# Head sums kept ungated, a gate's rows moved from TensorE to VectorE, and two moves in order, in a two-layer retention and neighbourhood-attention block

## The chip, the core and the metric

One NeuronCore of a Trainium2 chip runs the whole program. The metric is device time in microseconds (us) of one execution; the kernel before took 1186.53 us (median of 3 runs, 1186.47 to 1189.27). Engines are called as in the profile: PE is TensorE (PEld its weight loads), DVE is VectorE, ACT is ScalarE, POOL is GpSimd, SP is SyncE, which issues most DMAs (the trace marks rows of an issuing queue with a q, as in SPq).

## The reference

Two layers work on 256 latent rows `x` and 256 context rows `ctx` of width 1024. From a condition vector each layer gets six rows of modulation per stream (shift, scale and gate, twice), as `silu(c) @ ada_w + ada_b`. Layer 0 mixes by retention with 4 heads (query and key width 256, value width 512), layer 1 by neighbourhood attention with 32 heads; each is followed by a squared-ReLU MLP of width 4096. The lines that the change bears on:

```python
mod = silu_c @ ada_w[i] + ada_b[i]
sh1, sc1, g1, sh2, sc2, g2 = jnp.split(mod, 6, axis=-1)
h = x * (1.0 + sc1) + sh1
y, yc = retention_mixer(h, hc, ...)   # sum over 4 heads of (on * silu(g)) @ w_o
x = layer_norm(DN_ALPHA * x + g1 * y, ln_g[i, 0], ln_b[i, 0])
ctx = layer_norm(DN_ALPHA * ctx + g1c * yc, ln_g[i, 0], ln_b[i, 0])
```

## The kernel before

**Matmuls.** All matmuls of weights are done as three: weights and activations are each split into a high part (`hi`, cast by ACT) and a low part (`lo = raw - hi`, subtracted by DVE), and `mm3` adds hi·hi, hi·lo and lo·hi. Weights come in units of 512 KB through a ring of 4 raw buffers; `take` (line 322) keeps up to 5 split units ahead of PE. Every DMA of weights is issued by SP, in order. Eight PSUM banks serve all matmuls.

**Start.** Eight chunks of the model width are modulated one after the other. For a chunk, `chunk_sums` (854) forms its shift and scale rows on PE, `chunk_row` (869) copies them, `chunk_turn` (888) transposes the four row tiles of `x` and `ctx` into two halves of PSUM (tile `pt`, and a part of the bank `pada` that held the rows), `chunk_columns` (874) turns the rows into columns, and `chunk_modulate` (901) writes the modulated activations `hTh` and `hTl`, for ACT and DVE half each. `turn_over` (807) issues idle matmuls on a tile of ones (`still`). The transposed `x` and `ctx` stay in `R[0..3]`, two tiles of latent and two of context rows, 128 x 1024 each.

**Retention.** The loop over 4 heads stands at line 1045. For each head: projections of q and k (`proj_T`, tiles `pq`), of v (tiles `pv`), masked scores (`pS`, with decay tables in `strips`), the output gate (`gate`, `gates`, tiles `pg`), the attention output (`po`) with its normalisation on DVE and POOL, the turn to columns (`to_oT`, tiles `pT`), and the product with the output weights (`tok_mm`, tiles `pw`), eight tiles of 128 x 512 a head. Before the change `R` is scaled by ALPHA on ACT in head 0, and `accumulate` (756) of heads 0 to 2 multiplies each `pw` by the gate row `G1` on DVE (tile `acc`) and adds it to `R` on POOL.

**Modulation in the background.** The other modulation rows come from `bg_stream` (535), a generator that loads 512 KB of `ada_w` a step (tile `rawa`) and is advanced by calls of `bg()` at fixed places in the code. For most rows a step multiplies by the condition on DVE (`weigh`, 521: four operations of 128 x 512 into spare columns of `strips`), a reduction folds the sums (`folded`, 459, tile `red`), and one small PE product finishes them (`ada_columns`, `ada_gate`, tiles `pada`). The first gate row, item `(0, 0, 2)` of the plan, is done on PE instead: `ada_mm` (440) issues four column-tiled f32 matmuls a step, eight steps, all in head 0, and the row goes to DRAM and comes back as `G1` on POOL's queue. Weighing operations keep their place in the program's order on DVE; most other instructions are ordered by a scheduler.

**Attention of layer 1.** `STEPS` (1840) is a table of 13 steps. Its first two numbers say how many weight units are fetched (cast on ACT, subtracted on DVE) before `scores(n + 2)` and `soften(n + 2)` of the step, and how many behind them; the third fetches behind `flip` and `invert`. Then come the step's own products (`K`, `Q`, `V`, tiles `pn`, `pnv`), the transposes of `flip` (tiles `ppt`, copied to `pt` by ACT and DVE in turn) and `attend` (`pav`). `soften` (1591) is four reductions on DVE (tile `mn`, custom operations in the trace, ISA in the order of instructions) and four exponentials on ACT (tile `s`). Scores are the tiles `pqk`, four banks a step.

Of the kernel before, what the change touches and what calls it, by code (L numbers as in the profile page):

```python
# [17 lines left out]
P = 128  # L18
# [86 lines left out]
def kernel(  # L105
# [323 lines left out]

    def ada_bias(l, offs, nb):  # L430
        brow = scr("brow")
        ab = ada_b[l]
        for i in range(2):
            sp.dma_start(
                out=brow[64 * i : 64 * i + 64, :nb],
                in_=bass.AP(ab.tensor, ab.offset + offs[i], [[nb, 2], [0, 32], [1, nb]]),
            )
        return brow

    def ada_mm(pr, k, nb, rhs):  # L440

        lhsT = cT[:, k, :, :].rearrange("p a t -> p (a t)")
        for j in range(4):
            pe.matmul(
                pr[32 * j : 32 * j + 32, 0:nb],
                lhsT=lhsT,
                rhs=rhs(j),
                start=(k == 0),
                stop=(k == KC - 1),
                tile_position=(0, 32 * j),  # L450
            )

    def ada_row(pr, brow, nb, p0=0, p1=P, row=None):
        if row is None:
            row = smp.tile([P, 256], F32, tag="row", name=nm("row"), bufs=1)
        dve.tensor_add(out=row[p0:p1, :nb], in0=pr[p0:p1, 0:nb], in1=brow[p0:p1, :nb])
        return row

    def folded(red, acc, t, c0, n):
# [48 lines left out]

    def on_pe(l, w, part):
        return (l, w, part) == (0, 0, 2)  # L510

    def bg_load(l, w, part, offs, n):

        if l == 1 or w == 0:
# [20 lines left out]
    def bg_stream():  # L535
# [3 lines left out]
        for l, w, part in (  # L539
            [(0, 0, 2), (0, 1, 0), (0, 1, 1), (0, 1, 2)]  # L540
            + [(1, 0, 0), (1, 0, 1), (1, 0, 2), (1, 1, 0), (1, 1, 1), (1, 1, 2)]
        ):
            sh, sc, g = 3 * w * D, (3 * w + 1) * D, (3 * w + 2) * D
            offs = (sh + 512 * part, sc + 512 * part) if part < 2 else (g, g + 512)
            for n in range(KC):
                plan.append((l, w, part, offs, n))
        nxt = bg_load(*plan[0])
        yield
        for step, (l, w, part, offs, n) in enumerate(plan):
            raw = nxt  # L550
            if step + 1 < len(plan):
                nxt = bg_load(*plan[step + 1])

            nt = 2 if l == 0 or (w == 0 and part < 2) else 1
            if on_pe(l, w, part):
                if n == 0:
                    pr = bank("pada")
                if n == KC - 2:
                    brow = ada_bias(l, offs, 256)
                ada_mm(pr, n, 256, lambda j: raw[:, j // 2, (j % 2) * 256 : (j % 2 + 1) * 256])  # L560
                if n == KC - 1:
                    row = ada_row(pr, brow, 256)
                    for t in range(2):
                        pool.dma_start(
                            out=grow[l, w][t].rearrange("(j c) -> j c", j=4), in_=row[t:P:32, :]
                        )
                yield
                continue
            if n == 0:
                red = smp.tile([P, 2, 32], F32, tag="red", name=nm("red"), bufs=2)  # L570
            if l == 0:
                dve.on = True
                for kk in range(2):
                    for t in range(nt):
                        weigh(spare(t), raw[:, kk, :], t, 2 * (n % 4) + kk, n % 4 == 0 and kk == 0)
                dve.on = False
                if n % 4 == 3:
                    yield
                    for t in range(nt):
                        folded(red, spare(t), t, 512 * (n // 4), 512)  # L580
            else:
                if n == 0:
                    acc = slot(S_VL, [P, 2, D], F32, "acc")
                for t in range(nt):

                    dve.on = n == 0 and (w, part) == (0, 0)
                    weigh(acc[:, t], raw[:].rearrange("p a n -> p (a n)"), t, n, n == 0)
                    dve.on = False
                if n == KC - 1:
                    for t in range(nt):  # L590
                        folded(red, acc[:, t], t, 0, D)
            if n == KC - 1:
                if part < 2:
                    due.append(lambda a=(l, w, red, 4 * part, nt): ada_columns(*a))
                else:
                    due.append(lambda a=(l, w, red, nt): ada_gate(*a))
            yield
# [4 lines left out]

    bg_max = [39]

# [282 lines left out]

    def chunk_turn(k):

        pts[k] = bank("pt")[:, 0:256], prs[k][:, 256:512]  # L890
        for t in range(4):
            pe.transpose(pts[k][t // 2][:, tsl(t % 2)], R[t][:, tsl(k)], ident)
# [51 lines left out]
    chunk_row(0, tsl(1))  # L944
    chunk_turn(0)
    chunk_columns(0)
    turn_over(4)
    w = ws[0]
# [71 lines left out]

    def proj_T(th, tl, first=False):
        pb = [bank("pq") for _ in range(2)]
        for u in range(2):
            ((wh, wl),) = take(1)
            for dc in range(2):
                for kk in range(4):
                    k = 4 * u + kk
                    mm3(pb[dc][:], (wh[:, kk, tsl(dc)], wl[:, kk, tsl(dc)]), hs(k, 0, NT), k == 0, k == KC - 1)
            if first:
                bg(2)  # L1030
        rotate(pb, th, tl)
# [5 lines left out]

    G1s = [None]

    def first_gate():  # L1040

        if G1s[0] is None and bg_done[0] >= 9:
            G1s[0] = load_gate(0, 0, eng=nc.gpsimd)

    for h in range(RH):
        last = h == RH - 1
        if h == 0:
# [5 lines left out]
            evac_v(pv, vh, vl)  # L1053
            act.on = True
            for a in range(2):
                act.mul(out=RR[a][:], in_=RR[a][:], mul=ALPHA)
            act.on = False
            proj_T(qkh[:, 2:4], qkl[:, 2:4], True)
        else:
            qkh = slot(S_TH, [P, 4, NT], F32R, "qkh")  # L1060
            qkl = slot(S_TL, [P, 4, NT], F32R, "qkl")
            proj_T(qkh[:, 0:2], qkl[:, 0:2])
            proj_T(qkh[:, 2:4], qkl[:, 2:4])
            vh = slot(S_VH, [P, 4, DV], F32R, "vh")
            vl = slot(S_VL, [P, 4, DV], F32R, "vl")
            pv = [bank("pv") for _ in range(4)]
            for u in range(4):
                ((wh, wl),) = take(1)
                for t in range(4):
                    for kk in range(2):  # L1070
                        k = 2 * u + kk
                        mm3(pv[t][:], hs(k, t * P, (t + 1) * P), (wh[:, kk, :], wl[:, kk, :]), k == 0, k == KC - 1)
                bg()
            evac_v(pv, vh, vl)
        qh, ql, kh, kl = qkh[:, 0:2], qkl[:, 0:2], qkh[:, 2:4], qkl[:, 2:4]

        gs = slot(S_GS, [P, 4, DV], F32, "gs")
        gu = take(4)

        def gates(ts, between=()):  # L1080

            pgs = [bank("pg") for _ in ts]
            for k in range(KC):
                wh, wl = gu[k // 2]
                for t, pg in zip(ts, pgs):
                    mm3(pg[:], hs(k, t * P, (t + 1) * P), (wh[:, k % 2, :], wl[:, k % 2, :]), k == 0, k == KC - 1)
                if h == 0 and k == 3 and len(ts) == 1:
                    bg(2)
                    first_gate()
                if k in between:  # L1090
                    between[k]()
            return pgs

        def gate(t):
            return gates((t,))[0]

# [32 lines left out]
        if h == 0:  # L1129
# [3 lines left out]
            bg()  # L1133
            first_gate()
            pg = gate(1)
            act.activation(out=gs[:, 1, :], in_=pg[:], func=AF.Silu)
        else:
            S = masked_scores()
            for t in range(2):
                pg = gate(t)  # L1140
                act.activation(out=gs[:, t, :], in_=pg[:], func=AF.Silu)
                bg()
        ons = []
        for t in range(4):
# [14 lines left out]
            if t < 2:  # L1159
                pool.tensor_mul(out=gs[:, t, :], in0=on, in1=gs[:, t, :])  # L1160
            if h == 0 and t == 0:
                bg_until(9)
                first_gate()
                bg()
# [13 lines left out]

        between = {4: lambda: to_oT(0), 5: lambda: to_oT(1)}
        for t, pg in zip((2, 3), gates((2, 3), between)):  # L1180
            sg = scr("sg")
            act.activation(out=sg[:], in_=pg[:], func=AF.Silu)
            pool.tensor_mul(out=gs[:, t, :], in0=sg[:], in1=gs[:, t, :])

        bg_until(9)
        first_gate()
        G1 = G1s[0]

# [7 lines left out]
        def tok(t, half, us):  # L1196
            accumulate(tok_mm(t, half, us), t, half, G1)

# [9 lines left out]
        else:  # L1208
            bg_until(39)
            wus = take(4)  # L1210
# [101 lines left out]
    for hf in range(2):  # L1312
# [9 lines left out]
        if hf == 0:  # L1322
# [34 lines left out]
            outside()  # L1357
        bg_max[0] = 87
        for fp in range(len(hid), 8):
# [18 lines left out]
        for half in range(2):  # L1378
# [23 lines left out]
            bg_until(87)  # L1402
            held = take(4)
# [427 lines left out]
    def W(half, t):  # L1831
# [417 lines left out]
```

## Time and profile before

| | before |
|---|---|
| median of 3 runs | 1186.53 us |
| profiled execution: its time, its span | 1188.31 us, 1186.5 us |
| start and chunks | 0 to 56 us |
| retention | 56 to 450 us |
| first MLP | 450 to 800 us |
| attention, with its lead-in | 800 to 1000 us |
| second MLP | 1000 to 1186.5 us |
| instructions | 17867 |

The stages are set by the tiles at work. A row of the timeline gives start, duration, engine, operation, output and inputs, shapes and a count, and in brackets the idle time of the engine ahead of it with what ended it. Matmuls overlap: what a matmul costs PE is the distance from its start to the next start, not its duration.

### The profile page before, as it was taken

How to read it: one execution, taken by the hardware profiler on the slowest of the kernel's cores; microseconds unless marked ns; L12 is line 12 of the kernel's file. 1: busy time of each engine (PE TensorE's matmuls, PEld its weight loads, DVE VectorE, ACT ScalarE, POOL GpSimd, SP SyncE). 2: the span in 40 equal slices, each digit the busy share in tenths (PEclk: the TensorE clock that was granted, in tenths of full speed). 3: DMA queues.
4: the chain of work that ended last, by engine and by line, in shares of the span. 5: the costliest groups of instructions: out<-in, count | busy, mean ns of one | idle time of the engine just before them, and what ended most of it. 6: DMA issues, size and time to landing. Idle time of an engine off the chain costs nothing.

```text
span 1186.5 us, 17867 instructions
## 1 busy us (share of the span) xinstructions
PE 1176.7 (99%) x6884; PEld 990.9 (84%) x6884; DVE 832.8 (70%) x1304; ACT 480.9 (41%) x813; POOL 248.9 (21%) x389
## 2 busy tenths in 40 slices
PE   9999999999999999999999999999999999999997
PEld 7778888888888889888888888889888878999886
DVE  3876975886688487757876675668467588876446
ACT  3652222322223246441212333137466666665341
POOL 0104301310330141780202000223344430000001
PEclk9999999999999999999999999999999999999999
DMA  9964441444254216756566665637244434765660
GB/s 276 273 234 161 142 158 56 143 130 137 89 160 160 77 55 209 203 112 215 177 193 211 200 213 185 206 108 215 69 143 125 118 122 152 224 201 185 227 212 36
DMA packets 138041, 193.16 MB, mean 163 GB/s; under 512 B 9772, under 2 KB 81108, under 8 KB 137956
## 3 DMA queue, kind: packets, MB, share of 16 engines
q1 hardware_dynamic: 129572, 179.02, 47.3%
q0 software_dynamic: 7232, 10.44, 3.9%
q10 hardware_dynamic: 1152, 2.56, 0.7%
q8 instruction: 54, 0.88, 0.3%
q14 instruction: 31, 0.25, 0.1%
HBM read 187.15 MB, written 5.75 MB: 163 GB/s over the span
## 4 chain that ended last, share of the span: by engine, by line
PE 96%; ACT 1%; DVE 1%; issue 1%; DMA 0%; POOL 0%; DVEq 0%; ACTq 0%
PE p L84 44%; PE pq L84 8%; PE pg L84 7%; PE pv L84 7%; PE pw L84 7%; PE pn L84 5%; PE pnv L84 4%; PE po L84 3%; PE pada L84 2%; PE pnw L84 1%; PE pS L84 1%; PE ppt L84 1%; PE pqk L84 1%; PE pt L84 1%; PE pav L84 1%; PE p1t L84 1%
## 5 line engine op out<-in xcount | busy, mean ns | idle before, releaser
L84 ACT CAST hi<-raw 128x1024 fp32r<-128x1024 f32 (+2 forms) x228 | 232.7, 1032 | 325.0 <-PE p L84 151.3
L84 DVE TENSOR_TENSOR lo<-raw,hi 128x1024 fp32r<-128x1024 f32 (+2 forms) x228 | 280.3, 1240 | 101.8 <-ACT hi L84 101.0
L84 PE MATMUL p<-hi,hid 128*128 128x512 f32 (+1 forms) x832 | 241.8, 374 | 0.0
L84 PEld LDWEIGHTS p<-hi,hid 128*128 128x128 f32 x832 | 152.1, 188 | 27.7
L84 PE MATMUL p<-hTh,lo 128*128 128x256 f32 (+1 forms) x512 | 166.9, 329 | 0.0
L84 PE MATMUL p<-hTl,hi 128*128 128x256 f32 (+1 forms) x512 | 166.9, 329 | 0.0
L84 PE MATMUL p<-hTh,hi 128*128 128x256 f32 (+1 forms) x512 | 164.0, 330 | 0.0
L84 PE MATMUL p<-lo,hid 128*128 128x512 f32 (+1 forms) x416 | 155.3, 373 | 0.0
L84 DVE SCALAR_TENSOR_TENSOR acc<-rawa,scol,acc 128x1024 f32<-128x1024 f32 x56 | 74.7, 1344 | 63.1 <-DMA rawa<-in_ada_w_dram 62.9
L84 POOL TENSOR_TENSOR R<-R,acc 128x512 f32<-128x512 f32 x40 | 62.2, 1565 | 212.3 <-DVE acc L84 212.2
L84 PEld LDWEIGHTS p<-hTl,hi 128*128 128x128 f32 x512 | 96.4, 188 | 8.7
L84 PEld LDWEIGHTS p<-hTh,lo 128*128 128x128 f32 x512 | 96.3, 188 | 8.8
L84 PEld LDWEIGHTS p<-hTh,hi 128*128 128x128 f32 x512 | 95.1, 190 | 8.7
L84 PEld LDWEIGHTS p<-lo,hid 128*128 128x128 f32 x416 | 78.4, 188 | 13.6
L84 ACT CAST hid<-r 128x256 fp32r<-128x256 f32 (+1 forms) x64 | 31.9, 500 | 103.4 <-DVE r L84 103.3
L84 DVE SCALAR_TENSOR_TENSOR strips<-rawa,scol,strips 128x512 f32<-128x512 f32 x84 | 66.4, 847 | 0.0
L84 POOL TENSOR_TENSOR rstd<-rstd,misc 128x1 f32<-128x1 f32 x28 | 19.2, 686 | 215.5 <-DVE rstd L84 214.3
L84 ACT ACTIVATE s<-s,mn 128x512 f32<-128x512 f32 x64 | 45.5, 712 | 26.2 <-DVE mn L84 26.1
L84 PE MATMUL pg<-hi,hTh 128*128 128x512 f32 x128 | 51.1, 399 | 0.0
L84 PE MATMUL pw<-hi,oh 128*128 128x512 f32 x128 | 50.9, 398 | 0.0
L84 PE MATMUL pg<-lo,hTh 128*128 128x512 f32 x128 | 50.0, 391 | 0.0
L84 PE MATMUL pw<-hi,ol 128*128 128x512 f32 x128 | 50.0, 390 | 0.0
(238 smaller groups left out, 2277.1 us busy)
## 6 DMA issues: line engine op xcount, KB each, us to landing
raw<-in_mlp_w_dram SPq DMA_DIRECT2D x128, 512.0 KB, 4.2
rawa<-in_ada_w_dram SPq DMA_DIRECT2D x80, 512.0 KB, 4.3
raw<-in_ret_w_in_dram SPq DMA_DIRECT2D x42, 512.0 KB, 3.6
raw<-in_nat_w_in_dram SPq DMA_DIRECT2D x24, 512.0 KB, 3.9
rawq<-in_ada_w_dram SPq DMA_DIRECT2D x16, 512.0 KB, 5.8
raw<-in_ret_w_o_dram SPq DMA_DIRECT2D x16, 512.0 KB, 4.4
bias<-rpb_rows POOLq DMA_DIRECT2D x32, 128.0 KB, 2.9
raw<-in_nat_w_o_dram SPq DMA_DIRECT2D x8, 512.0 KB, 4.1
```

The costliest lines, as they stand in the source:

```text
L84: r = f(*args, **kwargs)
```

## The change

- **First gate on DVE.** `ada_bias`, `ada_mm`, `ada_row` and `on_pe` go. Item `(0, 0, 2)` is weighed on DVE as the other layer-0 items are; `bg()` calls are placed anew, and the counts 39 and 87 become 41 and 89. The four layer-0 items end in head 3 in both.
- **Head sums.** Head 0 copies each `pw` to `R` on ACT; heads 1 and 2 add `pw` to `R` on DVE. No POOL add and no gate is left in these. In head 3, `residual_in` reads `x` and `ctx` again by DMA (tile `xin`) and forms `G1 * R + ALPHA * x` on DVE, 2 operations for each of 8 half tiles. Head 3's own products are gated and added as before. `G1` is loaded on SP's queue.
- **First chunk.** Its second pair of transposes stands behind `chunk_columns`, in a PSUM bank of its own, and one `turn_over` matmul less follows.
- **Attention.** Steps 1 to 5 of the table fetch behind `soften`, and one unit of step 5 moves to the end of step 4.

```diff
-    def on_pe(l, w, part):
-        return (l, w, part) == (0, 0, 2)
+    EARLY = (0, 0, 2), (0, 1, 0), (0, 1, 1), (0, 1, 2)
...
-            if on_pe(l, w, part):
-                if n == 0:
-                    pr = bank("pada")
...
-                ada_mm(pr, n, 256, lambda j: raw[:, j // 2, (j % 2) * 256 : (j % 2 + 1) * 256])
-                if n == KC - 1:
-                    row = ada_row(pr, brow, 256)
-                    for t in range(2):
-                        pool.dma_start(
-                            out=grow[l, w][t].rearrange("(j c) -> j c", j=4), in_=row[t:P:32, :]
-                        )
...
-    def chunk_turn(k):
-
-        pts[k] = bank("pt")[:, 0:256], prs[k][:, 256:512]
-        for t in range(4):
+    def chunk_turn(k, ts=range(4)):
+
+        if k not in pts:
+            pts[k] = bank("pt")[:, 0:256], (prs[k][:, 256:512] if k else bank("pt")[:, 0:256])
+        for t in ts:
             pe.transpose(pts[k][t // 2][:, tsl(t % 2)], R[t][:, tsl(k)], ident)
...
-    chunk_turn(0)
+    chunk_turn(0, (0, 1))
     chunk_columns(0)
-    turn_over(4)
+    chunk_turn(0, (2, 3))
+    turn_over(3)
...
+    def residual_in(t):
+
+        for half in range(2):
+            sl = slice(half * 512, (half + 1) * 512)
+            xin = scr("xin")
+            sp.dma_start(out=xin[:], in_=(x, ctx_in)[t // 2][0][tsl(t % 2), sl])
+            dve.tensor_mul(out=R[t][:, sl], in0=R[t][:, sl], in1=G1[:, t // 2, sl])
+            dve.scalar_tensor_tensor(
+                out=R[t][:, sl], in0=xin[:], scalar=ALPHA, in1=R[t][:, sl], op0=ALU.mult, op1=ALU.add
+            )
...
-            for a in range(2):
-                act.mul(out=RR[a][:], in_=RR[a][:], mul=ALPHA)
...
+            if h == 2:
+                G1 = load_gate(0, 0, eng=nc.sync)
+            if last:
+                residual_in(0)
             proj_T(qkh[:, 0:2], qkl[:, 0:2])
+            if last:
+                residual_in(1)
+            else:
+                bg()
...
+                if last and u == 1:
+                    residual_in(2)
...
+        if last:
+            between[1] = lambda: residual_in(3)
...
         def tok(t, half, us):
-            accumulate(tok_mm(t, half, us), t, half, G1)
+            ps = tok_mm(t, half, us)
+            o = R[t][:, half * 512 : (half + 1) * 512]
+            if h == 0:
+                act.copy(out=o, in_=ps[:])
+            else:
+                dve.tensor_add(out=o, in0=ps[:], in1=o)
...
         (1, 0, 0, [K(2)], []),
-        (2, 0, 0, [K(3)], []),
-        (2, 0, 0, [K(4)], []),
-        (1, 0, 0, [K(5)], []),
-        (2, 0, 0, [Q(2)], []),
-        (1, 1, 0, [V(0)], []),
+        (0, 2, 0, [K(3)], []),
+        (0, 2, 0, [K(4)], []),
+        (0, 1, 0, [K(5)], []),
+        (0, 2, 1, [Q(2)], []),
+        (0, 1, 0, [V(0)], []),
```

PE, in the first chunk: the piece of the difference between the transposes (`pt`, `pada` from `R`), the columns (`pada` from `row`) and the first product of the q projection.

```order
 L84 MATMUL pt_205<-cst_81,R_104 128x128 x2
-L84 MATMUL pada_177<-cst_81,R_105 128x128 x2
 L84 MATMUL pada_177<-cst_81,row_186 128x2 x2
-L84 MATMUL pq_116<-still_95 128x256 x4
+L84 MATMUL pt_206<-cst_81,R_105 128x128 x2
+L84 MATMUL pq_116<-still_95 128x256 x3
```

The columns now stand ahead of the context rows' transposes, which write to a bank of their own.

PE, in head 0, at the end of the k projection (`pq`) and the begin of the first output gate (`pg`), before:

```order
L84 MATMUL pq_793<-hTh,hi_718 128x512
L84 MATMUL pq_793<-hTl,hi_718 128x512
L84 MATMUL pq_793<-hTh,lo_719 128x512
L84 MATMUL pada_828<-rawa_826,cT 32x256 x4
L84 MATMUL pada_828<-rawa_863,cT 32x256 x4
L84 MATMUL pg_900<-hi_750,hTh 128x512
L84 MATMUL pg_900<-lo_751,hTh 128x512
```

and now:

```order
L84 MATMUL pq_791<-hTh,hi_718 128x512
L84 MATMUL pq_791<-hTl,hi_718 128x512
L84 MATMUL pq_791<-hTh,lo_719 128x512
L84 MATMUL pg_879<-hi_750,hTh 128x512
L84 MATMUL pg_879<-lo_751,hTh 128x512
```

All eight `pada` rows of `ada_mm` are gone from head 0; a single product for the gate (`pada` from `red`) stands behind head 1's v projection.

DVE, in the attention step of `K(4)`, from the last values of the step before (`rt`, `oTl`) on, before:

```order
L84 TENSOR_TENSOR rt_7324<-pav_6956,rt_7324 128x128
L84 TENSOR_TENSOR oTl_6958<-rt_7324,oTh_6957 128x4x32
L84 TENSOR_TENSOR lo_7453<-raw_7450,hi_7452 128x1024
L84 TENSOR_TENSOR lo_7458<-raw_7455,hi_7457 128x1024
L84 ISA s_7480,mn_7478<-pqk_7462,bias_6872 128x512
L84 ISA mn_7478 128x1
```

and now the end of that step's softening:

```order
L84 ISA s_7464,mn_7453<-pqk_7440,bias_6859 128x512
L84 ISA mn_7453 128x1
L84 TENSOR_TENSOR lo_7470<-raw_7467,hi_7469 128x1024
L84 TENSOR_TENSOR lo_7475<-raw_7472,hi_7474 128x1024
L84 TENSOR_TENSOR kT_7479<-pn_7480,kT_7479 128x512
L84 COPY pt_6947<-ppt_7512 128x384
```

The two subtractions stood ahead of the four reductions and stand behind them now, right ahead of the evacuation of the keys (`kT`) and the copies of the transposes (`pt`). On ACT the two casts have moved in the same way, from ahead of the exponentials to behind them.

DVE, in the products with the output weights at the end of head 2, now:

```order
L84 TENSOR_TENSOR R_104<-pw_2751,R_104 128x512
L84 TENSOR_TENSOR R_104<-R_104,G_2118 128x512
L84 TENSOR_TENSOR ol_2656<-pT_2765,oh_2655 128x4x128
L84 SCALAR_TENSOR_TENSOR R_104<-xin_2918,R_104 128x512
L84 TENSOR_TENSOR R_104<-pw_2772,R_104 128x512
L84 TENSOR_TENSOR R_104<-R_104,G_2118 128x512
```

where before there stood `acc_2814<-pw_2801,G_1022`, `ol`, `acc_2837<-pw_2824,G_1022` and `ol`. The scheduler has drawn the first operations of `residual_in` forward from head 3: an operation that needs a DMA from `x` now stands among those that empty PSUM.

SP, at the same place, now:

```order
L84 DMA raw_2745<-in_ret_w_in_dram 128x4x256
L84 DMA rawa_2793<-in_ada_w_dram 128x2x512
L84 DMA raw_2829<-in_ret_w_in_dram 128x4x256
L84 DMA xin_2918<-in_x_dram 128x512
L84 DMA xin_2922<-in_x_dram 128x512
L84 DMA raw_2835<-in_ret_w_in_dram 128x4x256
```

The two new transfers stand between the two weight units of head 3's q projection.

More of the change, by code (lines that the diff above doesn't have):

```diff
@@ L428, in ada_load @@
         return raw
[L430 to L436, printed above, removed]
-            )
[L438 to L457, printed above, removed]
     def folded(red, acc, t, c0, n):
@@ L507, in ada_gate @@
             )
-    def on_pe(l, w, part):
-        return (l, w, part) == (0, 0, 2)
+    EARLY = (0, 0, 2), (0, 1, 0), (0, 1, 1), (0, 1, 2)
     def bg_load(l, w, part, offs, n):
-        if l == 1 or w == 0:
+        if (l, w, part) not in EARLY:
             return ada_load(l, n, offs)
@@ L539, in bg_stream @@
         for l, w, part in (
-            [(0, 0, 2), (0, 1, 0), (0, 1, 1), (0, 1, 2)]
+            list(EARLY)
             + [(1, 0, 0), (1, 0, 1), (1, 0, 2), (1, 1, 0), (1, 1, 1), (1, 1, 2)]
@@ L554, in bg_stream @@
             nt = 2 if l == 0 or (w == 0 and part < 2) else 1
-            if on_pe(l, w, part):
-                if n == 0:
-                    pr = bank("pada")
-                if n == KC - 2:
-                    brow = ada_bias(l, offs, 256)
-                ada_mm(pr, n, 256, lambda j: raw[:, j // 2, (j % 2) * 256 : (j % 2 + 1) * 256])
-                if n == KC - 1:
-                    row = ada_row(pr, brow, 256)
-                    for t in range(2):
-                        pool.dma_start(
-                            out=grow[l, w][t].rearrange("(j c) -> j c", j=4), in_=row[t:P:32, :]
-                        )
-                yield
-                continue
             if n == 0:
                 red = smp.tile([P, 2, 32], F32, tag="red", name=nm("red"), bufs=2)
-            if l == 0:
+            if (l, w, part) in EARLY:
                 dve.on = True
@@ L600 @@
     bg_done = [0]
-    bg_max = [39]
+    bg_max = [41]
     def bg(n=1):
@@ L1019, in rotate, with proj_T @@
             act.on = False
-    def proj_T(th, tl, first=False):
+    def proj_T(th, tl):
         pb = [bank("pq") for _ in range(2)]
@@ L1028, in proj_T @@
                     mm3(pb[dc][:], (wh[:, kk, tsl(dc)], wl[:, kk, tsl(dc)]), hs(k, 0, NT), k == 0, k == KC - 1)
-            if first:
-                bg(2)
         rotate(pb, th, tl)
@@ L1036, in evac_v @@
             dve.tensor_sub(out=vl[:, t, :], in0=pv[t][:], in1=vh[:, t, :].bitcast(F32))
[L1038 to L1043, printed above, removed]
+    def residual_in(t):
[7 more added lines that the diff above has]
+            )
     for h in range(RH):
@@ L1053 @@
             evac_v(pv, vh, vl)
-            act.on = True
-            for a in range(2):
-                act.mul(out=RR[a][:], in_=RR[a][:], mul=ALPHA)
-            act.on = False
-            proj_T(qkh[:, 2:4], qkl[:, 2:4], True)
+            proj_T(qkh[:, 2:4], qkl[:, 2:4])
         else:
@@ L1078 @@
         gu = take(4)
+        if h == 0:
+            bg()
         def gates(ts, between=()):
@@ L1086, in gates @@
                     mm3(pg[:], hs(k, t * P, (t + 1) * P), (wh[:, k % 2, :], wl[:, k % 2, :]), k == 0, k == KC - 1)
-                if h == 0 and k == 3 and len(ts) == 1:
-                    bg(2)
-                    first_gate()
                 if k in between:
@@ L1092, in gates, with gate @@
             return pgs
-        def gate(t):
-            return gates((t,))[0]
+        def gate(t, between=()):
+            return gates((t,), between)[0]
         def masked_scores():
@@ L1133 @@
             bg()
-            first_gate()
             pg = gate(1)
@@ L1139 @@
             for t in range(2):
-                pg = gate(t)
+                pg = gate(t, {} if t else {3: bg})
                 act.activation(out=gs[:, t, :], in_=pg[:], func=AF.Silu)
@@ L1160 @@
                 pool.tensor_mul(out=gs[:, t, :], in0=on, in1=gs[:, t, :])
-            if h == 0 and t == 0:
-                bg_until(9)
-                first_gate()
+            if t == 0:
                 bg()
@@ L1183 @@
             pool.tensor_mul(out=gs[:, t, :], in0=sg[:], in1=gs[:, t, :])
-        bg_until(9)
-        first_gate()
-        G1 = G1s[0]
         def tok_mm(t, half, us):
@@ L1196, in tok @@
         def tok(t, half, us):
-            accumulate(tok_mm(t, half, us), t, half, G1)
+            ps = tok_mm(t, half, us)
+            o = R[t][:, half * 512 : (half + 1) * 512]
+            if h == 0:
+                act.copy(out=o, in_=ps[:])
+            else:
+                dve.tensor_add(out=o, in0=ps[:], in1=o)
         if not last:
@@ L1208 @@
         else:
-            bg_until(39)
+            bg_until(41)
             wus = take(4)
@@ L1357 @@
             outside()
-        bg_max[0] = 87
+        bg_max[0] = 89
         for fp in range(len(hid), 8):
@@ L1401 @@
                 continue
-            bg_until(87)
+            bg_until(89)
             held = take(4)
```

## The prediction

> **What bounds the kernel now.** I read the page first: busy shares, granted clock, chain.
>
> ```profile
> PE 1176.7 (99%) x6884; PEld 990.9 (84%) x6884; DVE 832.8 (70%) x1304; ACT 480.9 (41%) x813; POOL 248.9 (21%) x389
> PEclk9999999999999999999999999999999999999999
> PE 96%; ACT 1%; DVE 1%; issue 1%; DMA 0%; POOL 0%; DVEq 0%; ACTq 0%
> ```
>
> TensorE is busy 99% of the span at its full clock, and 96% of the chain that ended last is TensorE's own work. So nearly every PE instruction that goes gives back its pitch, and work on another engine costs nothing until PE waits for it. What remains is to price the PE instructions, and to ask at which places another engine ends last. For that I read the timeline of PE around the removed groups, of PE, ACT and DVE in the attention steps, and the groups of DVE in the retention.
>
> The sum is made against the profiled execution: 1188.31 us, its span 1186.5 and 1.8 around it. The median of three runs, 1186.53, lies 1.8 below that; I subtract the same terms from it.
>
> **The change part by part.**
>
> *First gate off PE.* The tile view of `pada` and three places of PE's timeline (one ordinary matmul's row is left out in each, at the dots):
>
> ```profile
> L84 PE MATMUL pada<-rawa,cT x64: 379/379/403, 65.6 to 88.5; 128*32 128x256 f32 x64
> ```
> ```profile
> 65.25 0.39 PE L84 MATMUL pq<-hTh,lo 128*128 128x512 f32 x1
> 65.57 0.64 PE L84 MATMUL pada<-rawa,cT 128*32 128x256 f32 x8
> ...
> 66.47 0.39 PE L84 MATMUL pq<-hTl,hi 128*128 128x512 f32 x1
> ```
> ```profile
> 71.49 0.39 PE L84 MATMUL pq<-hTh,lo 128*128 128x512 f32 x1
> 71.81 1.07 PE L84 MATMUL pada<-rawa,cT 128*32 128x256 f32 x16
> ...
> 73.15 0.40 PE L84 MATMUL pg<-lo,hTh 128*128 128x512 f32 x1
> ```
> ```profile
> 416.10 0.39 PE L84 MATMUL pg<-hi,hTl 128*128 128x512 f32 x1
> 416.41 0.30 PE L84 MATMUL pada<-red,cst 128*32 128x64 f32 x2
> ...
> 416.98 0.39 PE L84 MATMUL pw<-lo,oh 128*128 128x512 f32 x1
> ```
> ```profile
> 337.77 0.39 PE L84 MATMUL pq<-hTh,hi 128*128 128x512 f32 x1
> 348.65 0.39 PE L84 MATMUL pq<-hTh,hi 128*128 128x512 f32 x1
> ```
>
> The last two rows are the first matmuls of two projections that follow one another without a stop; one projection is 48 matmuls, so a matmul's pitch is 10.88 / 48 = 0.227 us. From 65.25 to 66.47 lie 1.22 us and two matmuls: eight column-tiled ones cost 1.22 - 0.454 = 0.77. From 71.49 to 73.15 it is 1.66 - 0.454 = 1.21 for sixteen. The 64 stand as four groups of eight and two of sixteen: 4 x 0.77 + 2 x 1.21 = 5.49 us. The gate now needs one product like that of 416.41: 0.88 - 0.454 = 0.43. Together **-5.06 us**, all of it on the chain, since PE waits for nothing between these rows. If half of the gaps around a group stayed, for another reason than the group, it would be -2.5; nothing in the rows says so.
>
> *First chunk.* PE's start, and ACT in chunk 2:
>
> ```profile
> 9.28 0.51 PE L84 MATMUL pada<-cst,row 128*128 128x2 f32 x4
> 10.71 0.70 PE L84 MATMUL pq<-hTh,hi 128*128 128x512 f32 x2 [0.35 <-ACT hTh L84]
> ```
> ```profile
> 22.01 0.83 ACT L84 CAST hi<-raw 128x768 fp32r<-128x768 f32 x1 [4.46 <-DMA raw<-in_ret_w_in_dram]
> ```
>
> The columns leave up to 0.28 us earlier (not more: ahead of them stand two transposes instead of four, and they need the copied row), and so does the first product at 10.71, which waited 0.35 us for ACT. But at 22.01 ACT waits 4.46 us for a transfer of weights, and the cast that follows stands ahead of chunk 2's modulation; an earlier chunk waits for the same transfer. I take **0**, with bounds -0.28 and 0.
>
> *Attention, the fetches.* Scores of six steps on PE (the first is undisturbed), then ACT and DVE in the step of `K(4)`:
>
> ```profile
> 857.62 0.97 PE L84 MATMUL pqk<-kT,qT 32*128 32x512 f32 x12
> 866.74 1.11 PE L84 MATMUL pqk<-kT,qT 32*128 32x512 f32 x12
> 875.99 0.49 PE L84 MATMUL pqk<-kT,qT 32*128 32x512 f32 x2
> 876.82 1.31 PE L84 MATMUL pqk<-kT,qT 32*128 32x512 f32 x10 [0.34 <-ACT pt L84]
> 886.32 1.35 PE L84 MATMUL pqk<-kT,qT 32*128 32x512 f32 x12
> 896.09 1.71 PE L84 MATMUL pqk<-kT,qT 32*128 32x512 f32 x12
> 905.95 1.60 PE L84 MATMUL pqk<-kT,qT 32*128 32x512 f32 x12
> ```
> ```profile
> 868.91 2.00 ACT L84 CAST hi<-raw 128x1024 fp32r<-128x1024 f32 x2
> 875.83 0.56 ACT L84 CAST kT<-pn 128x512 fp32r<-128x512 f32 x1
> ```
> ```profile
> 869.99 2.36 DVE L84 TENSOR_TENSOR lo<-raw,hi 128x1024 fp32r<-128x1024 f32 x2 [0.82 <-ACT hi L84]
> 872.27 0.68 DVE L84 CUSTOM_DVE_ANT_1 s<-pqk,bias 128x512 f32<-128x512 f32 x1
> 876.43 0.69 DVE L84 TENSOR_TENSOR kT<-pn,kT 128x512 fp32r<-128x512 f32 x1 [1.63 <-ACT kT L84]
> ```
>
> Twelve score products take 0.97 us when nothing holds them. The later groups lose 0.14, 1.16 (875.99 to 878.13), 0.38, 0.74 and 0.63: 3.05 us in all, which is the most that can be won. They wait for banks that copies of `pt` empty on ACT and DVE, and these copies stand behind the keys' evacuation. Now the reductions need not wait for the subtractions: they begin near 869.2 instead of 872.27, and the exponentials end about 2.9 earlier, near 872.95. But the casts (2.00) follow them on ACT, and the subtractions (2.36, half a pair behind their cast) on DVE: ACT takes up the keys near 874.95 (0.9 earlier), DVE only near 876.3 (0.12 earlier), since its last subtraction ends there. DVE's copies hold the last bank, so the step gains 0.12, not 0.9. In the same way I get 0.14 for `K(3)`, 0.15 for `K(5)`, nothing for `Q(2)`, and 0.55 for `V(0)`, where a whole unit leaves the step: **-0.95 us**. Bounds: -3.05, all waits; and +0.7 if the two units fall full in the keys' way in two steps, by 0.35 each (the 0.34 that a group waits now).
>
> *DVE's load in the retention.* Windows (span, PE, PEld, DVE, ACT, POOL busy with counts, clock, DMA), groups from 100 to 420 us, and the unloaded subtraction from 60 to 100:
>
> ```profile
> 56.00:400.00 344.00, 344.00 (x1616) 281.39 (x1615) 256.84 (x388) 104.68 (x149) 64.72 (x67) 1.00 0.43 138
> ```
> ```profile
> L84 DVE TENSOR_TENSOR lo<-raw,hi 128x1024 fp32r<-128x1024 f32 x52 | 72.3, 1401 | 26.3 <-ACT hi L84 26.2
> L84 DVE TENSOR_TENSOR acc<-pw,G 128x512 f32<-128x512 f32 x24 | 16.0, 675 | 3.1 <-PE pw L84 3.1
> L84 DVE TRANSPOSE_TENSOR_REDUCE red<-strips 128x16 f32<-128x512 f32 x12 | 8.1, 689 | 0.0
> ```
> ```profile
> L84 DVE TENSOR_TENSOR lo<-raw,hi 128x1024 fp32r<-128x1024 f32 x5 | 5.9, 1218 | 2.0 <-ACT hi L84 2.0
> ```
> ```profile
> L84 DVE SCALAR_TENSOR_TENSOR strips<-rawa,scol,strips x84: 734/744/1785, 99.1 to 380.3; 128x512 f32<-128x512 f32 x84
> ```
>
> Added: 32 weighing operations at 0.744 (23.8 us), four folds at 0.69 (2.8), the gate's small ones (0.5), and `residual_in`, 8 x (0.68 + 0.744) = 11.4. Removed: eight products of head 0 at 0.675 (5.4), which are ACT copies now; in heads 1 and 2 an addition takes the place of a product of the same shape. That is +33, 290 of 344 us, 84% instead of 75%. Weighing ranges from 0.734 to 1.785 us and the subtraction from 1.22 to a mean of 1.40, beside the additions on POOL, 24 of 40 of which go. If that excess went wholly, 9 + 9 us would come back: 80%. On the path I take **0**: PE is busy through all of the window, and the cover is the split units that stand ahead of it. At its thinnest, where head 3 begins:
>
> ```profile
> 342.10 4.57 DVE L84 TENSOR_TENSOR lo<-raw,hi 128x1024 fp32r<-128x1024 f32 x3
> ```
>
> the first unit of the k projection is split by about 343.6, and PE takes it at 348.65: **5 us** of slack. Without that cover a late microsecond of DVE is a late microsecond of PE. The last gating on DVE in head 3 stays as it was. Bounds: 0 (a faster DVE wins nothing on a full PE) and, from rival E below, some +10.
>
> [...]
>
> *A new wait.* `residual_in` waits on DVE for `xin`, in head 2's last products and in head 3; behind it DVE holds subtractions of weights, the normalisation and the evacuations of `pw`, for all of which PE waits in the end. `xin` is not in the trace; its nearest rows (DMA busy in 40 slices of 29.7 us, and two transfers' sizes and landing times):
>
> ```profile
> DMA  9964441444254216756566665637244434765660
> ...
> R<-in_x_dram SPq DMA_DIRECT2D x8, 128.0 KB, 6.5
> raw<-in_ret_w_in_dram SPq DMA_DIRECT2D x42, 512.0 KB, 3.6
> ```
>
> A re-read of 256 KB should land between 3.6 and 6.5 us after its issue. Its issue stands ahead of DVE's need by more than a unit of weights (24 matmuls, 5.4 us of PE), and the 5 us of slack cover the rest: 0.
>
> **Sum.** -5.06 + 0 - 0.95 + 0 = -6.0: 1188.31 becomes 1182.3 in a profiled execution, and 1186.53 becomes **1180.5**.
>
> **The rivals.**
>
> - *A, the forecast, 0.58.* 1180.5; its own range is 1179.3 to 1182.0, from the attention between about -2.1 and +0.5.
> - *B, all waits of the scores go, 0.14.* -5.06 - 3.05 - 0.28 gives 1178.1. For it: the keys' cast on ACT is 0.9 earlier, and one group names ACT's `pt`. Against: DVE's subtractions stand right ahead of its own `kT`.
> - *C, the attention's new order doesn't do what it says, 0.10.* The fetch only changes its place in the step, and holds the copies of `pt` as the softening did, or longer: -5.06 + 0.7 gives 1182.2.
> - *D, DVE at 84% reaches PE in places, 0.11.* Two to four short waits where the weights or a `pw` come late, 1.5 to 4.5 us in all: 1182 to 1185. For it: the slack of 5 us is five or six DVE operations. Against: DVE idles 26 us in the group of subtractions alone, waiting for casts.
> - *E, slower: DVE stands still for `xin`, 0.07.* Four places, one for each `residual_in`, with up to three loads of 512 KB ahead in SP's order. Each costs what its wait exceeds 5 us. At 7.5 us, 4 x 2.5 = 10 eats the 6.0 and more: 1190.5. It turns slower than before from a wait of 6.5 us each (4 x 1.5 = 6.0), and slower by a visible margin from 7.4 us. For it: small reads took 6.5 us to land in the start. Against: that was in the first slices, with DMA at 90% or more; it is at 43% in this window.
>
> [...]
>
> **How the numbers follow.** A measurement of this kernel tells about 0.3% from no change: 3.56 us, so 1182.97 and 1190.09 are the bounds. Faster: A, B, nine tenths of C and some of D, 0.83; same: the rest of C and D and a little of E, 0.11; slower: most of E, 0.06. The range goes from B, 1178.0, to the end of D, 1185.0; it leaves out E and a little of each side.
>
> **What would show it.** Right: no `pada` from `rawa`, and the first MLP's `p` begins 5 us earlier; PE without idle rows from 56 to 450; weighing nearer to 0.744 on the mean, additions on POOL 16 instead of 40; the groups of `pqk` shorter by some 0.1 each and the last by 0.5, DVE's `kT` waiting for its own subtractions, not for ACT. Start: chunk 2's first `hTh` at the same time as before. Wrong: PE idle for ACT `hi`, DVE `lo` or `pw` in heads 2 and 3 (D), with DVE idle ahead of `R` from `xin` by DMA (E); `pqk` groups at 0.97 (B) or longer than before (C).

## The result and the profile after

| | before | after |
|---|---|---|
| median of 6 runs | 1186.67 us | 1179.12 us |
| profiled execution: its time, its span | 1188.31, 1186.5 us | 1179.48, 1177.4 us |
| ratio of the times | | 0.9939 (0.9927 to 0.9951) |

The change takes 7.55 us off the median; 6.0 were forecast. The page after, in the lines that were shown of before:

```profile
PE 1167.3 (99%) x6821; PEld 985.6 (84%) x6821; DVE 844.6 (72%) x1349; ACT 480.6 (41%) x819; POOL 212.5 (18%) x364
PEclk9999999999999999999999999999999999999999
PE 94%; DMA 2%; SPq 1%; ACT 1%; DVE 1%; issue 0%; POOL 0%; ACTq 0%; DVEq 0%
```

The kernel is bound as it was. PE's busy time fell by 9.4 us, but that is not all the change's. In the second MLP, which the change doesn't touch, 40 us of the profiled execution held 342 matmuls before and 355 after (window, busy times with counts, clock, DMA share, GB/s):

```profile
1040.00:1080.00 40.00, 40.00 (x342) 40.00 (x341) 29.14 (x45) 24.79 (x43) 0.00 (x0) 1.00 0.60 189
```
```profile
1033.50:1073.50 40.00, 40.00 (x355) 40.00 (x354) 30.17 (x47) 23.87 (x44) 0.00 (x0) 1.00 0.61 191
```

Two executions of one and the same kernel can differ like this: one of the variants below was profiled twice, with 356 matmuls from 1035 to 1075 us in one execution and 342 in the other. Over the last 624 of these matmuls the two paces are 2.76 us apart (73.57 and 70.81 us). The times of single runs cluster in the same way, those of the kernel before near 1186.5 and 1189.1, of the changed one near 1178.6 and 1181.6; that the clusters are these paces is inferred, since only a profiled execution shows its pace. The profile of before caught the slow pace, that of after the quick one. So of the 9.1 us between the two spans some 2.8 belong to the draw, and the comparison is made stage by stage, from a matmul of before to the same matmul of after. The stages below account for the spans: +0.75 at the start, -5.27, -1.75 and the pace's -2.76 make 9.0 of the 9.1.

**Retention**, from the last products of the start to head 3's first projection, before and after:

```profile
55.67 0.70 PE L84 MATMUL pq<-hTh,hi 128*128 128x512 f32 x2
337.77 0.39 PE L84 MATMUL pq<-hTh,hi 128*128 128x512 f32 x1
```
```profile
56.42 0.47 PE L84 MATMUL pq<-hTh,hi 128*128 128x512 f32 x1
333.25 0.39 PE L84 MATMUL pq<-hTh,hi 128*128 128x512 f32 x1
```

282.10 us became 276.83: 5.27 less. This stretch hardly varies with the new gate (276.77 to 277.00 us in seven profiles of the changed kernel and its variants below, 277.34 where DVE was loaded further); with the old gate, in the kernel before and three variants of it, it took 282.10 to 283.42. Where sixteen products of `ada_mm` stood behind the k projection, the gate's matmuls now follow at their pitch:

```profile
71.44 0.39 PE L84 MATMUL pq<-hTh,lo 128*128 128x512 f32 x1
71.67 0.39 PE L84 MATMUL pg<-hi,hTh 128*128 128x512 f32 x1
```

**Attention**, the scores of the same six steps:

```profile
853.08 0.97 PE L84 MATMUL pqk<-kT,qT 32*128 32x512 f32 x12
862.20 0.97 PE L84 MATMUL pqk<-kT,qT 32*128 32x512 f32 x12
871.31 1.12 PE L84 MATMUL pqk<-kT,qT 32*128 32x512 f32 x12
880.59 1.47 PE L84 MATMUL pqk<-kT,qT 32*128 32x512 f32 x12
890.48 1.61 PE L84 MATMUL pqk<-kT,qT 32*128 32x512 f32 x12
900.23 0.98 PE L84 MATMUL pqk<-kT,qT 32*128 32x512 f32 x12
```

The first two lose nothing, the others 0.15, 0.50, 0.64 and 0.01 us: 1.30 in all where it was 3.05, so 1.75 less. The step of `K(4)` gave 1.01 of it, `V(0)` 0.62; `K(5)` lost 0.12 more than before.

**Start.** The first product leaves at 10.16 instead of 10.71, now behind a wait of 0.38 us for DVE's `hTh` in place of 0.35 for ACT's. Not all of this is the order's doing: over all profiles it leaves from 10.38 to 10.81 in the old order (three profiles) and from 10.16 to 10.80 in the new one (ten). Chunk 2's `hTh` on ACT starts at 23.02 instead of 22.90, behind the same wait for weights:

```profile
22.19 0.83 ACT L84 CAST hi<-raw 128x768 fp32r<-128x768 f32 x1 [4.91 <-DMA raw<-in_ret_w_in_dram]
23.02 0.56 ACT L84 ACTIVATE hTh<-pt,mod 128x256 fp32r<-128x256 f32 x1
```

Later in the start, this execution falls behind: the products of another chunk begin at 37.40 instead of 36.67, after PE waited 0.46 us for ACT's `hTh`, and so the retention begins 0.75 us later (56.42 instead of 55.67).

**DVE in the retention**: the same window, and groups from 96 to 416 us:

```profile
56.00:400.00 344.00, 344.00 (x1577) 284.59 (x1576) 271.16 (x437) 106.42 (x156) 31.04 (x47) 1.00 0.46 145
```
```profile
L84 DVE SCALAR_TENSOR_TENSOR strips<-rawa,scol,strips 128x512 f32<-128x512 f32 x107 | 74.1, 754 | 0.0
L84 DVE TENSOR_TENSOR lo<-raw,hi 128x1024 fp32r<-128x1024 f32 x52 | 66.3, 1281 | 31.3 <-ACT hi L84 31.3
L84 DVE SCALAR_TENSOR_TENSOR R<-xin,R 128x512 f32<-128x512 f32 x8 | 5.3, 681 | 0.2 <-DMA xin<-in_x_dram 0.2
```

DVE is busy 14.3 us more, 79% of the window, and PE still waits for nothing in it. Of the eight operations that need `xin`, one waited, 0.2 us; a transfer took 3.9 to 5.3 us to land.

### The profile page after: what moved, and what is told of

Read it like the earlier page. It is cut to its first block, busy times and chain, and to the rows that moved or that the text cites. A ratio compares the mean times of both kernels' runs of the same rounds, so it can differ in the third digit from the quotient of the medians.

```text
span 1177.4 us, 17745 instructions
## 1 busy us (share of the span) xinstructions
PE 1167.3 (99%) x6821; PEld 985.6 (84%) x6821; DVE 844.6 (72%) x1349; ACT 480.6 (41%) x819; POOL 212.5 (18%) x364
## 4 chain that ended last, share of the span: by engine, by line
PE 94%; DMA 2%; SPq 1%; ACT 1%; DVE 1%; issue 0%; POOL 0%; ACTq 0%; DVEq 0%
PE p L84 44%; PE pw L84 7%; PE pg L84 7%; PE pq L84 7%; PE pv L84 7%; PE pn L84 5%; PE pnv L84 4%; PE po L84 3%; PE ppt L84 2%; PE pnw L84 1%; PE pS L84 1%; PE pav L84 1%; PE pqk L84 1%; SPq L84 1%; PE pt L84 1%; PE p1t L84 1%
## 5 line engine op out<-in xcount | busy, mean ns | idle before, releaser
L84 DVE TENSOR_TENSOR lo<-raw,hi 128x1024 fp32r<-128x1024 f32 (+2 forms) x228 | 273.4, 1213 | 105.5 <-ACT hi L84 105.4
L84 DVE SCALAR_TENSOR_TENSOR strips<-rawa,scol,strips 128x512 f32<-128x512 f32 x112 | 78.6, 762 | 0.0
L84 POOL TENSOR_TENSOR R<-R,acc 128x512 f32<-128x512 f32 x16 | 25.8, 1633 | 168.8 <-DVE acc L84 168.8
L84 PE MATMUL pq<-hTh,hi 128*128 128x512 f32 x128 | 49.3, 395 | 0.8 <-ACT hTh L84 0.5
```

Of the source, the lines that this page charges most:

```text
L84: r = f(*args, **kwargs)
```

## The experiments

Times are medians; in brackets the ratio to the kernel before of the same chip, with its 95% interval.

**The attention's table alone.** The kernel before with the five new rows of `STEPS`.

> The kernel before with the attention table of the change and nothing else. By the trace of the changed kernel the six groups of scores lose 1.30 us where they lost 3.05, so this theory expects 1.75 us less than before, about 1184.8, with the group behind K(4) at 1.1 us instead of 2.1. My prediction's working, in which DVE's copies hold the last bank, expects 0.95 less, 1185.6. If the table does nothing, 1186.5.

Measured: 1184.65 us against 1186.74 (0.9971, 0.9959 to 0.9982): 2.1 less by the medians, 3.4 by the ratio. The two differ because the ten runs of this kernel lie close together (1183.95 to 1185.19) and those of before spread over 6 us; against the 18 of the 28 that lie below 1187.5 (median 1186.44) it is 1.8 less. The size is read from the trace: the scores behind `K(4)` took 0.97 us, those behind `K(5)` and `Q(2)` lost 0.68 and 0.63, and all together lost 1.7 less than before. The trace's sum, not the prediction's, holds. The group behind `K(5)` waits there 0.19 us for DVE's `kT`. This run's trace shows another thing, in the old gate's products:

```profile
80.34 0.64 PE L84 MATMUL pada<-rawa,cT 128*32 128x256 f32 x8 [1.27 <-DMA rawa<-in_ada_w_dram]
```

PE waits 1.27 us for the rows of the gate's weights. The profile of before has no such wait.

**The first chunk alone.** The kernel before with `chunk_turn` in two parts and `turn_over(3)`.

> The kernel before with the new order of the first chunk and nothing else. The prediction expects no change, 1186.5, since chunk 2 waits for a transfer. The rival: the first chunk's gain of 0.3 to 0.55 us, which the changed kernel's trace shows at 11.7 us, reaches the end and with it comes part of the 1.5 us by which the changed kernel is faster than forecast: 1185.5 to 1186.2. A second rival: the later loss of 0.7 us at 36.7 us in that trace belongs to the new order, 1187.2.

Measured: 1186.60 against 1186.74 (1.0, 0.9988 to 1.0012): nothing that can be told from none, as forecast. Here too PE waits for `rawa`, 1.16 us at 80.34. The loss at 36.7 us does not go with the order: a second profile of the changed kernel (below) is there at 36.39, before the old one's 36.67, and this run's at 36.89.

**The first gate back on PE.** The changed kernel with `ada_mm` and the counts 39 and 87 again.

```diff
+    def on_pe(l, w, part):
+        return (l, w, part) == (0, 0, 2)
...
-        if (l, w, part) not in EARLY:
+        if (l, w, part) not in EARLY or on_pe(l, w, part):
...
+            if on_pe(l, w, part):
...
+                ada_mm(pr, n, 256, lambda j: raw[:, j // 2, (j % 2) * 256 : (j % 2 + 1) * 256])
```

> The changed kernel with the first gate's 64 column-tiled products back on PE, and the head sums still ungated. If the gain of the retention is those products, eight groups of eight at 0.77 us come back and the gate's own product of 0.43 goes: 5.7 us more than the changed kernel, 1184.8. If the gain comes from the ungated sums (POOL's additions gone, DVE less blocked), nothing comes back: 1179.1.

Measured: 1184.60 (0.9981, 0.9971 to 0.9990), 5.5 above the changed kernel. From the last products of the start to head 3 PE takes 282.77 us, 5.94 more than the changed kernel, and the time is that of the attention's table alone on the same chip, 1184.65. So the retention's gain is the products that left PE. The ungated sums give nothing themselves; by the code they make room for the move, since no gate is needed before head 3.

**POOL's additions back.**

```diff
-                dve.tensor_add(out=o, in0=ps[:], in1=o)
+                acc = scr("acc")
+                dve.tensor_copy(out=acc[:], in_=ps[:])
+                pool.tensor_add(out=o, in0=o, in1=acc[:])
```

> The changed kernel, but heads 1 and 2 copy each product from PSUM on DVE and add it to R on POOL, as the kernel before does with gated products: 16 additions on POOL come back. DVE's cover theory expects the same time as the changed kernel, 1179.1 within 0.5, with the subtraction of 128x1024 in the retention going back from a mean of 1.28 us towards 1.40 and the weighing from 0.75 towards 0.85. If the new order leaves DVE no slack, the 10 or so us of DVE time that come back show as 1 to 5 us more.

Measured: 1179.14 (0.9939, 0.9921 to 0.9957), the changed kernel's time. DVE's groups in it:

```profile
L84 DVE SCALAR_TENSOR_TENSOR strips<-rawa,scol,strips 128x512 f32<-128x512 f32 x107 | 79.9, 808 | 0.0
L84 DVE TENSOR_TENSOR lo<-raw,hi 128x1024 fp32r<-128x1024 f32 x52 | 67.6, 1308 | 25.8 <-ACT hi L84 25.8
```

Sixteen additions on POOL lengthen 107 weighing operations from 754 to 808 ns and 52 subtractions from 1281 to 1308: 5.8 and 1.3 us of DVE, none of it on the path.

**Only the subtractions behind the softening.** The changed kernel, with the casts of steps 1 to 5 in front again.

```diff
-        fetch(early)
+        split_ = n in (1, 2, 3, 4, 5)
+        fetch(late if split_ else early)
         lows(early)
         scores(n + 2)
         soften(n + 2)
-        fetch(late)
+        fetch(0 if split_ else late)
         lows(late)
```

> The changed kernel with one thing undone in the attention steps 1 to 5: the casts on ACT stand ahead of the softening again, as before; only the subtractions on DVE stay behind it. ACT then reaches the keys as soon as in the changed kernel, and DVE's subtractions need not wait 2.1 us for a cast any more. If DVE's copies hold the last bank, as the prediction worked it, the scores of all steps come to 0.97 us and the time is 1.0 to 1.3 below the changed kernel, near 1178. If ACT's copies hold the bank and the exponentials end later behind the casts, the steps of K(4) and K(5) lose again what they won, 1 us or more above the changed kernel.

Measured: 1177.57 against 1186.19 (0.9927, 0.9915 to 0.9940). The scores behind the steps of `K(4)`, `K(5)`, `Q(2)` and `V(0)`, and DVE in the step of `K(4)`:

```profile
870.39 0.97 PE L84 MATMUL pqk<-kT,qT 32*128 32x512 f32 x12
879.51 0.97 PE L84 MATMUL pqk<-kT,qT 32*128 32x512 f32 x12
888.90 0.97 PE L84 MATMUL pqk<-kT,qT 32*128 32x512 f32 x12
898.01 0.97 PE L84 MATMUL pqk<-kT,qT 32*128 32x512 f32 x12
```
```profile
865.34 2.37 DVE L84 TENSOR_TENSOR lo<-raw,hi 128x1024 fp32r<-128x1024 f32 x2
868.57 0.69 DVE L84 TENSOR_TENSOR kT<-pn,kT 128x512 fp32r<-128x512 f32 x1 [0.86 <-ACT kT L84]
```

The subtractions start right behind the last reduction, are done 0.86 us before the keys can be taken, and the scores, 1.1 us after that, find all banks free. In the changed kernel the same step reads, on DVE and on ACT:

```profile
869.27 2.36 DVE L84 TENSOR_TENSOR lo<-raw,hi 128x1024 fp32r<-128x1024 f32 x2 [2.10 <-ACT hi L84]
871.55 0.68 DVE L84 TENSOR_TENSOR kT<-pn,kT 128x512 fp32r<-128x512 f32 x1
```
```profile
868.21 1.98 ACT L84 CAST hi<-raw 128x1024 fp32r<-128x1024 f32 x2
870.10 0.57 ACT L84 CAST kT<-pn 128x512 fp32r<-128x512 f32 x1
870.57 0.84 ACT L84 COPY pt<-ppt 128x384 f32<-128x384 f32 x2
```

In the changed kernel DVE idles 2.10 us for a cast that the change itself put behind the exponentials, and then goes from the subtractions straight to the keys.

**The same in the kernel before.**

```diff
         fetch(early)
-        lows(early)
+        behind = early if n in (1, 2, 3, 4, 5) else 0
+        lows(early - behind)
         scores(n + 2)
         soften(n + 2)
+        lows(behind)
```

> The kernel before with its own attention table, its casts ahead of the softening and its units where they were; only the subtractions of steps 1 to 5 stand behind the softening. If it is the subtractions ahead of the reductions that make the scores wait, all but the unit of V(0)'s step comes back: the groups of scores at 0.97 us, 2.4 to 3.1 us less than before, 1183.1 to 1183.8. If the casts on ACT and the moved unit count, it gains less than the changed table alone, 2.1 us.

Measured: 1183.88 against 1187.28 (0.9973, 0.9961 to 0.9985): 3.2 less by the ratio, 3.4 by the medians, with every group of scores at 0.97 us. Moving the subtractions alone wins all of the 3.05 us, so their place ahead of the reductions was the cause; with the casts and the unit moved as well, 1.3 us of it stay lost in the groups. The times don't tell these two tables apart (the ratio of the first was 0.9971, of this one 0.9973); the traces do.

**Side by side.** The changed kernel, and the one with only the subtractions behind, on one chip.

> The changed kernel once more, beside the next run on one chip: 1179.1.

> The changed kernel with the casts ahead of the softening and the subtractions behind it, once more, beside the run before on one chip: 1.1 to 1.4 us below it, by the attention's groups of scores, which came to 0.97 us in all steps.

Measured: 1179.88 (0.9940, 0.9925 to 0.9955) and 1180.19 (0.9935, 0.9920 to 0.9950). The times of this pair don't tell them apart; 1.1 to 1.4 us between them were expected. Each kernel's six runs spread over 4.6 to 5.4 us, and of the two profiled executions the first ran the second MLP at the quick pace, the second at the slow one. The traces do tell them apart: from the scores behind `K(4)` to those of the step after `V(0)` it is 870.72 to 908.81 us in the one and 870.02 to 906.76 in the other, 38.09 and 36.74, so 1.35 less. From 423.70 to 1009.24 and from 422.94 to 1007.41, between the two MLPs, it is 1.07 less, since the second execution loses some 0.2 us again behind these steps. With the earlier runs of both the medians are 1179.1 (12 runs) and 1177.85 (11 runs), over different chips. I take the version as about 1 us better than the changed kernel, by its trace.

**DVE at 90%.** In each weighing step two needless maxima of a sum with itself.

```diff
+                        if t == 0:
+                            dve.tensor_tensor(out=spare(t), in0=spare(t), in1=spare(t), op=ALU.max)
```

> The changed kernel with 64 needless operations of 128x512 on DVE (the maximum of a weighing sum with itself), two in each of the 32 weighing steps of the retention: some 44 us of DVE work more, from 79% to about 92%. If DVE's load alone made late weights or late evacuations (rival D, which put this at 84%), PE would wait in heads 1 to 3 and the time rises by 1.5 to 4.5 us. If the split units ahead of PE cover it, the time stays within 0.5 us of the changed kernel.

Measured: 1180.07 (0.9948, 0.9933 to 0.9963), 1 us above the changed kernel. The window, and the longest of PE's waits:

```profile
56.00:400.00 344.00, 343.77 (x1575) 284.37 (x1574) 310.85 (x497) 105.27 (x154) 37.21 (x45) 1.00 0.44 143
```
```profile
PE pt L84 <- ACT xn L84: 1.7, 1, 1.7
```

At 90% of the window the weights still come in time. What is late is the normalisation behind head 3 (`xn`), for which PE waits 1.7 us at the retention's end: DVE reaches the last `acc` later there. The place has no room in the changed kernel either: in its second profile PE waits 0.46 us there, in its first not at all.

**A stall of DVE**, 7.6 and 18.3 us long, behind the operations of `xin` between head 3's q and k projections.

```diff
+                dve.on = True
+                dve.tensor_reduce(
+                    out=scr("idle")[:, 0:14], in_=spare(0).unsqueeze(1).broadcast_to([P, 14, 512]),
+                    axis=mybir.AxisListType.X, op=ALU.max,
+                )
+                dve.on = False
```

(34 in the place of 14 for the longer one.)

> The changed kernel with one needless operation on DVE, about 7 us long, between the second pair of additions of xin and the next subtraction in head 3: a wait of that length, as rival E has it, at the place that I took for the thinnest. With the 5 us of slack that the prediction reads there, PE waits 2.5 us and so does the end. By the order of the instructions, which names the unit that this subtraction serves, PE takes that unit 17.5 us behind it; then nothing changes.

Measured: 1178.99 (0.9940, 0.9926 to 0.9953): nothing.

> As the run before it, with an operation of about 18 us. With 5 us of slack PE waits 13 us. With 17.5 us of slack PE waits 1 to 4 us, for that unit's subtraction or for the evacuated keys that stand behind it.

Measured: 1189.97 (1.0038, 1.0020 to 1.0056), 10.9 above the changed kernel. The operation on DVE, and the matmul that waited:

```profile
349.94 18.28 DVE L84 TENSOR_REDUCE idle<-strips 128x34 f32<-128x17408 f32 x1
```
```profile
389.17 0.79 PE L84 MATMUL pg<-hi,hTh 128*128 128x512 f32 x1 [8.87 <-DVE vl L84]
```

Neither 5 us nor the 17.5 that were expected for the next unit of weights was the slack: that unit was split by 369.4, and PE waited for no weights. PE stopped for the evacuated values (`vl`), which stand far behind the stall in DVE's queue; what was covered is 18.28 - 8.87 = 9.4 us. From 349.94 to 368.14 us the trace has no other operation on DVE. The one that held it computes; none that waits 7 us for a transfer was run, so what such a wait costs was not shown.

## Why the prediction was right, step by step

- **First gate off PE, -5.06: right.** The trace gives -5.27 between like matmuls, and putting the products back costs 5.5 us of time and 5.94 of the retention. One sentence of the step failed: "PE waits for nothing between these rows". It was true of the one profiled execution of before; in two other profiles with the old gate PE waits 1.16 and 1.27 us there for `rawa`, in a third 0.3. Where that wait occurs it goes with the products, and the sum had no term for it.
- **First chunk, 0: right**, in the time (1.0, 0.9988 to 1.0012) and in the way: the first product left earlier (by 0.55 us in this pair, with a spread of 0.4 to 0.6 within either order) and chunk 2 started no earlier.
- **Attention, -0.95: right in sign, half of the size.** It is -1.75 by the groups of scores and, by the run of its own, -1.8 to -3.4 depending on which runs of before are set against it. The step that failed is "DVE's copies hold the last bank, so the step gains 0.12, not 0.9". In the step of `K(4)` the row of before named ACT's `pt`, and the group followed ACT. Against the group of scores behind the step, ACT took up the keys 1.05 us earlier than before (1.21 us ahead of it instead of 0.16) and DVE 0.20 (0.24 behind it instead of 0.44), near the 0.9 and 0.12 that were worked out; the group gained 1.01. So both engines' times were right, and the choice of the one that holds the bank was wrong. In `K(5)` and `Q(2)` DVE's subtractions do stand in the keys' way, as worked out, and 0.50 and 0.64 stay lost. Nearly all of 3.05 was there to be had (rival B's 3.05 is what the kernel with only its subtractions moved reaches), with the casts left in front.
- **DVE's load, 0 on the path: right.** Busy time rose by 14.3 us; the working had +33, or +15 if the excess beside POOL's additions went wholly, and the second is nearer: weighing fell from a mean of 849 ns (100 to 420 us of before) to 754, the subtraction from 1401 to 1281. With sixteen additions back on POOL the two means are 808 and 1308 ns. That this stays off the path is shown by the time with these additions, 1179.14. Rival D needs more than this: at 90% the loss is 1 us.
- **The slack of 5 us: wrong, by luck on the safe side.** By the order of instructions the unit split by 343.6 is the k projection's second, taken 5.4 us after 348.65: 10.5 us of slack. The stalls measured 9.4 us for head 3, bounded by an evacuation, not by weights. Rival E would decide beyond that, and `xin` lands in a median of 4.8; the new wait, put at 0, was 0.2 us on DVE and nothing on PE.
- **The sum.** -6.0 against -7.55. The result, 1179.12, lies below A's own range (1179.3 to 1182.0), between A and B; the whole range holds it because it reaches to B. The attention makes up 0.8 us of the difference, the retention 0.2, the wait for `rawa`, where it occurs, up to 1.3. How often it occurs in unprofiled runs stays open, and with it the rest of the difference.

## What to carry to other kernels

When an engine holds two kinds of work in one queue, look for the operation that others wait for least directly and put that one behind; here it was the subtraction alone, and taking its cast along gave 1.3 of 3.05 us back. Read a stage from two executions before calling it free of waits: a DMA that PE does not wait for in one can be a stall in another (here 0 us for `rawa` in the profile of before, and 0.3, 1.16 and 1.27 us in three others with the old gate). A slack is measured at every consumer behind an instruction, evacuations too; here it was an evacuation that was missed first, not the next unit of weights.

## What the runs showed of the hardware

- A stretch of 624 matmuls of 128x256, with weight loads busy all the time, runs at one of two paces from execution to execution of one kernel (342 or 355 matmuls in 40 us, at a granted clock of 1.00 in both windows; 342 and 356 in two executions of the variant with only its subtractions behind). Nothing in the runs says what sets it.
- After the stall of 8.87 us PE did not come back at full speed: in the 5.83 us behind it the granted clock was 0.62 and 17 matmuls ran where 26 fit at 0.227 us each, so the stall cost some 2 us more than its length.

```profile
389.17:395.00 5.83, 5.83 (x17) 4.63 (x18) 5.83 (x11) 2.80 (x5) 0.00 (x0) 0.62 0.64 218
395.00:402.24 7.24, 7.24 (x33) 5.98 (x32) 7.15 (x12) 0.82 (x2) 0.00 (x0) 1.00 0.22 76
```
